# The values of the block-sparse heads: one projection 512 columns wide in the place of two of 256

## The chip, the core and the metric

The kernel runs on one core of a Trainium2 chip. The metric is device time in microseconds (us), the median of several executions. TensorE is the engine that multiplies matrices, VectorE (DVE), ScalarE (ACT) and GpSimd (POOL) do the rest, and each works through its own list of instructions in order.

## The reference

Two transformer blocks run one after the other on 512 tokens of width 1024, in float32. The change is in the first block's projection, of which this is the part that matters:

```python
h = rms_norm(x, norm_mix_pre_g[l])
proj = h @ w_in[l]
mq, mk, mv, dq, dk, dv, ga, gb = jnp.split(proj, split_at, axis=-1)
...
ya = moba_attention(moba_heads(mq), moba_heads(mk), moba_heads(mv), moba_slopes)
...
yb = diff_attention(dq[:, :, 0], dq[:, :, 1], dk[:, :, 0], dk[:, :, 1], dv, lam, diff_slopes)
```

The block-sparse attention (`moba_attention`) has 8 heads of 64 columns, so that `mq`, `mk` and `mv` are 512 columns each. A query attends to its own block of 256 tokens and, where a gate allows, to the block before it. The gate is the sign of the query's product with the mean of the earlier block's keys. The differential attention (`diff_attention`) follows with 4 heads.

## The kernel before

Every product of float32 operands is made of three: each operand is split into a high and a low part (`split`: ScalarE copies the high part, VectorE subtracts it), and `mm3` (lines 371 to 373) adds high·high, high·low and low·high in PSUM. The weights come from memory as slabs. A slab is loaded into a raw tile `wr` (two tiles of 2048 columns) and split in pieces of 1024 columns into tiles `wh` and `wl`, of which there are four pairs (`halves_w`). A slab of 256 columns takes two pieces of four k-blocks each, and a slab of 512 columns takes four pieces of two k-blocks each. The splits of weights are issued at a high priority (`WPRIO`), so that they stand early in the queues of ScalarE and VectorE.

The first block's projections and attention heads share TensorE by a planner, `weave`, that writes TensorE's order down when the kernel is built. It has two lists. *Fills* are projections, taken strictly in the order of their list: `mq`, `mk`, `mv` of half 0 (four heads), the small constants, `mq`, `mk`, `mv` of half 1, then `dq`, `dk`, `dv` of each half, gates, and the branch products. *Chains* are the attention heads: at most three (`WIDTH1`) are active. Each step of a chain states how much it costs and how long the next step has to wait. Whenever a step of an active chain is due, it is taken; otherwise the current fill goes on; and if there is no fill that may start, the planner takes the chain step that comes due first and so TensorE's next instruction is one that waits. A fill may start only when the names that it requires are done: `dq` of half 0 requires `mot` 0 and `mot` 1, the last steps of the first two pairs of heads, because it takes over their tiles.

The heads go in pairs. For a pair p, `moba_open` (`mog`) multiplies the queries by the mean of the keys (line 828, the gate), `moba_head` (`mo`, two for a pair) makes the scores (line 615), the softmax (621 on VectorE, 623 on ScalarE), transposes the probabilities (line 753), splits them, multiplies them by the values (line 883), and folds the result (818, 819). `moba_tail` (`mot`) transposes the sums (line 896) and scales the result (897). `mog` needs `mq` and `mk` of its half, and `mo` needs `mog` and `mv` of its half. The keys' consumer `take_mk` fills the stacked keys on ScalarE and VectorE and then the means (lines 773 and 777), which the gate reads.

The values are projected with the tokens on the partitions: `fill_tok` multiplies each of four groups of 128 tokens by a slab of 256 columns, 24 matmuls a group, with two groups in one PSUM bank; `take_stack_v` then copies and splits the result into stacked tiles (809 and 810).

Of the kernel before, what the change touches and what calls it, by code (L numbers as in the profile page):

```python
# [18 lines left out]
P = 128  # L19
S = 512  # L20
D = 1024
KT = D // P
# [30 lines left out]
CPRIO = 300  # L53
# [24 lines left out]
def STEP(pe=0.0, dve=0.0, act=0.0, ops=(), lat=0.0, free=0, need=0, back=0):  # L78

    return Step(pe, dve, act, ops, lat, free, need, back)
# [11 lines left out]
def transformer_blocks_kernel(  # L94
# [51 lines left out]
    def nm(s):  # L146
        uid[0] += 1
        return f"{s}_{uid[0]}"

    def big(tag, bufs, dt=F32, cols=512):  # L150
        return sp.tile([P, cols], dt, tag=tag, bufs=bufs, name=nm(tag))
# [13 lines left out]
    def acc():  # L165
        return pa.tile([P, 512], F32, tag="a", name=nm("a"))
# [7 lines left out]
    def f32(t):  # L174
        return t.bitcast(F32)
# [90 lines left out]
    def wslab(src, kt, cols, later=None):  # L266
        return list(wpieces(src, kt, cols, later))
# [102 lines left out]
    def mm3(ps, lh, ll, rh, rl, first, last):  # L370
        T.matmul(ps, lh, rh, start=first, stop=False)  # L371
        T.matmul(ps, lh, rl, start=False, stop=False)  # L372
        T.matmul(ps, ll, rh, start=False, stop=last)  # L373
# [12 lines left out]
    def slab_tok(slab, kt, act, ntt, cols):  # L386

        for t in range(ntt):
            if t % 2 == 0:
                bank = acc()  # L390
            ps = bank[:, (t % 2) * 256:(t % 2) * 256 + cols]
            sl = slice(t * P, (t + 1) * P)
            for (k, n, hi, lo) in slab:
                for j in range(n):
                    ah, al = act[k + j]
                    mm3(ps, ah[:, sl], al[:, sl], hi[:, j, :], lo[:, j, :], k + j == 0, k + j == kt - 1)
            yield ps
# [170 lines left out]
    with tc.issue_after(pows[-1].ins):  # L568
        h, ready = pre.operand(w_in[0][:, :256])
# [16 lines left out]
    W1 = w_in[0]  # L586
# [63 lines left out]
    def fill_tok(W, c0, kt, ops, consume, dve, act):  # L650
        held = []
        slab = W if c0 is None else wslab(W[:, c0:c0 + 256], kt, 256)
        for g, ps in enumerate(slab_tok(slab, kt, ops, 4, 256)):
            yield STEP(pe=0.32 * kt, dve=0.28 * kt * (g == 3), act=0.24 * kt * (g == 3))
            held.append((g, ps))
            if g % 2:
                with tc.high_priority(CPRIO):
                    for args in held:
                        consume(*args)
                held = []  # L660
                yield STEP(dve=2 * dve, act=2 * act)

    def weave(chains, fills, width, banks, model):

        hop, bank_lat, fill_lat = model
        now = 0.0
        busy = {"D": [], "A": [], "G": []}  # L670
        done = {}
        banks = [0.0] * banks
        active, todo, queue, cur = [], list(chains), list(fills), None

        def place(engine, t, d):

            spans = busy[engine]
            spans[:] = [sp_ for sp_ in spans if sp_[1] > now]
            k = 0
            while k < len(spans) and spans[k][0] < t + d:  # L680
                t = max(t, spans[k][1])
                k += 1
            spans.insert(k, (t, t + d))
            return t + d

        def take(gen):
            nonlocal now
            st_ = next(gen)
            now += st_.pe
            ready_ = now  # L690
            for e, d in (("D", st_.dve), ("A", st_.act)):
                if d:
                    ready_ = max(ready_, place(e, now + hop, d))
            for ops in st_.ops:
                t = now
                for e, d in ops:
                    t = place(e, t + hop, d)
                ready_ = max(ready_, t)
            banks.extend([ready_ + bank_lat] * st_.free)
            banks.sort()  # L700
            del banks[:max(0, -st_.free)]
            return st_, max(ready_, now + st_.lat)

        def start(c):

            return max(c[2], banks[c[3] - 1] if c[3] else 0.0)

        while active or todo or queue or cur:
            for c in list(todo):
                if len(active) >= width:  # L710
                    break
                name, req, fn = c
                if all(r in done for r in req):
                    todo.remove(c)
                    gen = fn()
                    active.append([name, gen, max([done[r] for r in req] + [0.0]), next(gen).need, []])
            can = [c for c in active if c[3] <= len(banks)]
            due = [c for c in can if start(c) <= now]
            if not due:
                if cur is None and queue and all(r in done for r in queue[0][1]):  # L720
                    name, _, fn = queue.pop(0)
                    cur = [name, fn(), 0.0]
                if cur is not None:
                    try:
                        cur[2] = max(cur[2], take(cur[1])[1])
                    except StopIteration:
                        done[cur[0]] = max(now, cur[2]) + fill_lat
                        cur = None
                    continue
                due = [min(can, key=start)]  # L730
                now = max(now, start(due[0]))
            c = due[0]
            del banks[:c[3]]
            c[3] = 0
            try:
                st_, ready_ = take(c[1])
                c[4].append(ready_)
                c[2] = c[4][-1 - min(st_.back, len(c[4]) - 1)]
                c[3] = st_.need
            except StopIteration:  # L740
                done[c[0]] = c[2]
                active.remove(c)
# [61 lines left out]
    def take_stack_v(key, tag, half):  # L804
        def consume(g, ps):
            v = big(tag, 16, F32R)
            hi, lo = [v.rearrange("p (h u c) -> p h u c", u=2, c=64)[:, :, u] for u in range(2)]
            src = ps.rearrange("p (h c) -> p h c", c=64)
            A.copy(hi, src)
            V.tensor_tensor(lo, src, f32(hi), op=ALU.subtract)  # L810
            for m in range(2):
                store.setdefault((key, half * 2 + m), []).append([v[:, c:c + P] for c in (m * 256, m * 256 + P)])
        return consume
# [216 lines left out]
    fills, chains = [], []  # L1030
    old = []
    for half in range(2):
        tag = "qs"[half]
        c0 = half * 256
        fills.append((("mq", half), old, lambda c0=c0, tag=tag, half=half:
                      fill_feat(W1, c0, take_q("mq", -0.125, tag, half), 1.25, 1.0, DLAT)))
        fills.append((("mk", half), old, lambda c0=c0, tag=tag, half=half:
                      fill_feat(W1, 512 + c0, take_mk(tag, half), 2.4, 2.0, DLAT, half == 0)))
        fills.append((("mv", half), old, lambda c0=c0, tag=tag, half=half:
                      fill_tok(W1, 1024 + c0, KT, h, take_stack_v("mv", tag, half), 0.4, 0.3)))  # L1040
        for p_ in (2 * half, 2 * half + 1):
            chains.append((("mog", p_), [("mq", half), ("mk", half)], lambda p_=p_: moba_open(p_)))
            for hh in range(2):
                chains.append((("mo", p_, hh), [("mog", p_), ("mv", half)],
                               lambda p_=p_, hh=hh: moba_head(p_, hh)))
            chains.append((("mot", p_), [("mo", p_, 0), ("mo", p_, 1)], lambda p_=p_: moba_tail(p_)))
    fills.insert(3, (("gains",), [], fill_constants))
    for half in range(2):
        tag = "qs"[half]
        c0 = half * 256  # L1050
        old = [("mot", 2 * half), ("mot", 2 * half + 1)]
# [8 lines left out]
    for br in range(2):  # L1060
        old = [("di", 0), ("di", 1)] if br == 0 else [("di", hd) for hd in range(4)]
# [109 lines left out]
    h, ready = pre.operand(w_gate[0][:, :256], lambda: mem_slabs(range(0, MEM1)))  # L1171
# [142 lines left out]
    h, ready = pre.operand(ffn1_w_gu_2[0][:, :256], lambda: mem_slabs(range(MEM1, MEM2)))  # L1314
# [20 lines left out]
    h, ready = pre.operand(w_in_2[0][:, 2048:2304], lambda: mem_slabs(range(MEM2, 8)))  # L1335
# [234 lines left out]
    with tc.issue_after(load.ins):  # L1570
# [39 lines left out]
        fills, chains = [], []  # L1610
# [77 lines left out]
    h, ready = pre.operand(mem_w_q_2[0][:, :256])  # L1688


    mo = [None] * KT
# [72 lines left out]
    fills = [(("mq", hd), [], lambda hd=hd: fill_mq(hd)) for hd in range(4)]  # L1764
    fills.append((("mo",), [("ma", hd) for hd in range(3)], fill_mo))
    chains = [(("ma", hd), [("mq", hd)], lambda hd=hd: mem_head(hd)) for hd in range(4)]
# [4 lines left out]
    h, ready = pre.operand(ffn2_w_gu_2[0][:, :256])  # L1771
# [57 lines left out]
```

## Time and profile before

| | us |
|---|---|
| median of 3 runs | 1915.24 |
| lowest and highest | 1912.54, 1916.43 |
| the profiled execution: its time | 1915.45 |
| the profiled execution: its span, first to last instruction | 1913.7 |
| TensorE busy | 1881.5 |
| VectorE busy | 1387.2 |
| ScalarE busy | 929.2 |

The trace is of one execution, whose time of 1915.45 us is 1.75 us more than its span and 0.21 us above the median. Busy time of TensorE is from modelled ends that overlap the next start, so that a stretch without gaps is told better by the starts.

### The profile page before, as it was taken

What the parts mean: (1) busy time and instruction counts of PE and PEld (TensorE: products, weight loads), DVE (VectorE), ACT (ScalarE), POOL (GpSimd) and SP (SyncE); (2) the same over time, 40 slices, a digit from 0 to 9 for tenths busy, and PEclk for the clock granted to TensorE, in tenths of its full rate; (3) what the DMA queues carried; (4) which work ended last, traced back from release to release, by engine and by line L of the source; (5) the groups of instructions that cost most, each with busy time, mean ns of one, the idle gap of its engine ahead of it and who ended that gap; (6) DMA issues with size and microseconds to landing.
All of it is one profiled execution on the core that took longest, in us unless ns stands there. A gap on an engine that the chain in (4) does not pass through costs nothing.

```text
span 1913.7 us, 29312 instructions
## 1 busy us (share of the span) xinstructions
PE 1881.5 (98%) x11566; PEld 1688.7 (88%) x11566; DVE 1387.2 (72%) x2217; ACT 929.2 (49%) x1537; POOL 175.0 (9%) x272
## 2 busy tenths in 40 slices
PE   8999999999999999999999999999999999999998
PEld 7899888888999998889999988888978778999997
DVE  6777635468878786677878757888866448878785
ACT  5666534364544344444344456668555344344443
POOL 2240100050000002000000010330510000000000
PEclk9999999999999999999999999999989999999999
DMA  5221223462232324423232343211223222332322
GB/s 180 67 67 56 78 66 133 143 203 89 89 111 89 114 97 168 151 89 102 97 111 88 111 148 101 67 45 45 89 89 110 77 81 82 102 111 89 111 89 89
DMA packets 161452, 192.40 MB, mean 101 GB/s; under 512 B 7361, under 2 KB 131362, under 8 KB 161314
## 3 DMA queue, kind: packets, MB, share of 16 engines
q1 hardware_dynamic: 159746, 185.80, 29.8%
q0 software_dynamic: 1280, 4.20, 0.6%
q8 instruction: 91, 1.49, 0.3%
q10 hardware_dynamic: 288, 0.52, 0.1%
q14 instruction: 47, 0.39, 0.1%
HBM read 182.11 MB, written 8.39 MB: 100 GB/s over the span
## 4 chain that ended last, share of the span: by engine, by line
PE 88%; issue 5%; DVE 3%; ACT 2%; POOL 2%; POOLq 0%; ACTq 0%; DVEq 0%
PE b L372 16%; PE b L373 16%; PE b L371 16%; PE a L371 11%; PE a L372 11%; PE a L373 11%; PE a L513 4%; PE b L615 1%; PE b L1444 1%; PE b L489 1%; DVE wl L403 1%; PE b L753 1%; DVE w L1540 0%; ACT wh L402 0%; PE b L883 0%
## 5 line engine op out<-in xcount | busy, mean ns | idle before, releaser
L403 DVE TENSOR_TENSOR wl<-wr,wh 128x1024 fp32r<-128x1024 f32 (+1 forms) x381 | 463.5, 1220 | 269.9 <-ACT wh L402 266.1
L402 ACT CAST wh<-wr 128x1024 fp32r<-128x1024 f32 (+1 forms) x381 | 394.0, 1036 | 443.0 <-PE b L372 154.5
L371 PE MATMUL b<-wh,q 128*128 128x512 f32 x672 | 262.4, 390 | 0.0
L372 PE MATMUL b<-wl,q 128*128 128x512 f32 x672 | 262.0, 390 | 0.0
L373 PE MATMUL b<-wh,q 128*128 128x512 f32 x664 | 257.9, 389 | 0.0
L371 PE MATMUL a<-h,wh 128*128 128x512 f32 (+1 forms) x660 | 238.4, 361 | 0.0
L373 PE MATMUL a<-h,wl 128*128 128x512 f32 (+1 forms) x660 | 234.9, 356 | 0.0
L372 PE MATMUL a<-h,wh 128*128 128x512 f32 (+1 forms) x660 | 234.7, 356 | 0.0
L372 PE MATMUL b<-h,wh 128*128 128x256 f32 (+1 forms) x568 | 175.9, 310 | 0.0
L371 PE MATMUL b<-h,wh 128*128 128x256 f32 (+1 forms) x568 | 175.9, 310 | 0.0
L373 PE MATMUL b<-h,wl 128*128 128x256 f32 (+1 forms) x568 | 175.9, 310 | 0.0
L371 PEld LDWEIGHTS b<-wh,q 128*128 128x128 f32 x672 | 126.3, 188 | 24.7
L373 PEld LDWEIGHTS b<-wh,q 128*128 128x128 f32 x664 | 124.6, 188 | 26.5
L372 PEld LDWEIGHTS b<-wl,q 128*128 128x128 f32 x672 | 126.3, 188 | 24.3
L372 PE MATMUL a<-s,wh 128*128 128x256 f32 (+1 forms) x488 | 141.2, 289 | 0.0
L373 PEld LDWEIGHTS a<-h,wl 128*128 128x128 f32 x660 | 124.5, 189 | 18.3
L371 PEld LDWEIGHTS a<-h,wh 128*128 128x128 f32 x660 | 124.7, 189 | 17.9 <-issue 0.5
L372 PEld LDWEIGHTS a<-h,wh 128*128 128x128 f32 x660 | 124.8, 189 | 17.8 <-issue 0.5
L372 PEld LDWEIGHTS b<-h,wh 128*128 128x128 f32 x568 | 108.3, 191 | 5.6
L373 PEld LDWEIGHTS b<-h,wl 128*128 128x128 f32 x568 | 108.2, 191 | 5.6
L371 PEld LDWEIGHTS b<-h,wh 128*128 128x128 f32 x568 | 108.1, 190 | 5.6
L372 PEld LDWEIGHTS a<-s,wh 128*128 128x128 f32 x488 | 93.1, 191 | 1.3
(374 smaller groups left out, 4195.9 us busy)
## 6 DMA issues: line engine op xcount, KB each, us to landing
wr<-in_ffn_w_gu_dram SPq DMA_DIRECT2D x88, 512.0 KB
wr<-in_w_in_dram SPq DMA_DIRECT2D x68, 512.0 KB
wr<-in_ffn_w_down_dram SPq DMA_DIRECT2D x44, 512.0 KB
wr<-in_w_gate_dram SPq DMA_DIRECT2D x22, 512.0 KB
wr<-in_w_up_dram SPq DMA_DIRECT2D x22, 512.0 KB
wr<-in_w_down_dram SPq DMA_DIRECT2D x22, 512.0 KB
wr<-in_mem_w_kv_dram SPq DMA_DIRECT2D x16, 512.0 KB
wr<-in_w_out_dram SPq DMA_DIRECT2D x10, 512.0 KB
```

The lines of the kernel that those rows point to most:

```text
L371: T.matmul(ps, lh, rh, start=first, stop=False)
L372: T.matmul(ps, lh, rl, start=False, stop=False)
L373: T.matmul(ps, ll, rh, start=False, stop=last)
L402: A.copy(hi, src)
L403: V.tensor_tensor(lo, src, f32(hi), op=ALU.subtract)
L489: T.transpose(banks[k][:, t * P:(t + 1) * P], self.s[t, k // 4][:, (k % 4) * P:(k % 4 + 1) * P], ident)
L513: T.matmul(accs[m], lh, rh, start=c == 0 and n in (0, 2), stop=c == KT - 1 and n > 3)
L615: T.matmul(ps, lh[n], rh[n], start=n == 0, stop=n == 1)
L753: T.transpose(ps[:, o * P:(o + 1) * P], blk, ident)
L1444: T.matmul(ps[:, gg * 64:(gg + 1) * 64], e[:, gg * P:(gg + 1) * P], up, start=True, stop=True)
```

## The change

The two fills `mv` of half 0 and half 1 become one fill, in the place of the first. It loads a slab 512 columns wide and multiplies each of the four groups of tokens by it: 24 matmuls of 512 columns a group, each group in a PSUM bank of its own, which the consumers of the two halves read one after the other. All heads now require this one fill. The list of fills has one entry less between `mk` of half 1 and `dq` of half 0.

```diff
+    def fill_both(W, c0, consumes, dve, act):
+
+        slab = wslab(W[:, c0:c0 + 512], KT, 512)
+        for t in range(4):
+            ps = acc()
+            sl = slice(t * P, (t + 1) * P)
+            for (k, n, hi, lo) in slab:
+                for j in range(n):
+                    ah, al = h[k + j]
+                    mm3(ps, ah[:, sl], al[:, sl], hi[:, j, :], lo[:, j, :], k + j == 0, k + j == KT - 1)
+                yield STEP(pe=1.36, dve=1.13 * (t == 3), act=0.95 * (t == 3))
+            with tc.high_priority(CPRIO):
+                for half, consume in enumerate(consumes):
+                    consume(t, ps[:, half * 256:(half + 1) * 256])
+            yield STEP(dve=2 * dve, act=2 * act)
...
-        fills.append((("mv", half), old, lambda c0=c0, tag=tag, half=half:
-                      fill_tok(W1, 1024 + c0, KT, h, take_stack_v("mv", tag, half), 0.4, 0.3)))
+        if half == 0:
+            fills.append((("mv",), old, lambda:
+                          fill_both(W1, 1024, [take_stack_v("mv", "qs"[u], u) for u in range(2)], 0.4, 0.3)))
...
-                chains.append((("mo", p_, hh), [("mog", p_), ("mv", half)],
+                chains.append((("mo", p_, hh), [("mog", p_), ("mv",)],
```

## Rows read from the trace of the kernel before

**Rows 1.** The page's busy times: us (share of the span), instructions.

```profile
PE 1881.5 (98%) x11566; PEld 1688.7 (88%) x11566; DVE 1387.2 (72%) x2217; ACT 929.2 (49%) x1537; POOL 175.0 (9%) x272
```

**Rows 2.** Busy time in stretches of the first block: us busy (instructions), clock, DMA.

```profile
37.22:50.50 13.28, 13.28 (x113) 13.27 (x112) 7.52 (x24) 5.22 (x8) 5.96 (x8) 1.00 0.25 80
50.50:85.16 34.66, 34.66 (x190) 29.99 (x188) 27.51 (x71) 24.53 (x57) 11.36 (x13) 1.00 0.19 61
85.16:101.34 16.18, 15.84 (x131) 15.70 (x130) 11.13 (x32) 8.30 (x15) 4.59 (x6) 1.00 0.21 67
```

**Rows 3.** TensorE's waits in the whole span, this one of 14.

```profile
PE b L828 <- DVE c L777: 0.3, 1, 0.3
```

**Rows 4.** TensorE in order of time, where `mk` of half 0 and `mv` run.

```profile
26.34 0.39 PE L371 MATMUL b<-h,wh 128*128 128x512 f32 x1
...
37.22 0.28 PE L371 MATMUL a<-wh,h 128*128 128x256 f32 x1
...
40.09 0.28 PE L371 MATMUL a<-wh,h 128*128 128x256 f32 x1
```

**Rows 5.** The page's group of weight loads for 512-column products: busy us, mean ns.

```profile
L371 PEld LDWEIGHTS a<-h,wh 128*128 128x128 f32 x660 | 124.7, 189 | 17.9 <-issue 0.5
```

**Rows 6.** VectorE in order of time, a weight piece that `mk` of half 0 frees.

```profile
38.28 1.23 DVE L403 TENSOR_TENSOR wl<-wr,wh 128x1024 fp32r<-128x1024 f32 x1 [0.56 <-ACT wh L402]
```

**Rows 7.** TensorE in order of time from the last `mk` product to `dq`.

```profile
85.16 0.28 PE L371 MATMUL a<-wh,h 128*128 128x256 f32 x1
...
90.91 1.25 PE L753 MATMUL b<-ident,w 128*128 128x128 f32 x10
92.00 0.95 PE L828 MATMUL b<-c,s 128*128 128x1 f32 x8
93.29 1.08 PE L828 MATMUL b<-c,s 128*128 128x1 f32 x8 [0.34 <-DVE c L777]
...
97.18 1.40 PE L883 MATMUL b<-w,q 128*128 128x512 f32 x8
...
101.34 0.60 PE L896 MATMUL b<-ident,w 128*128 128x128 f32 x4
101.70 1.63 PE L615 MATMUL b<-s,s 128*128 128x128 f32 x12
103.16 0.40 PE L371 MATMUL a<-h,wh 128*128 128x512 f32 x1
```

**Rows 8.** VectorE in order of time after the last `mk` product.

```profile
85.18 1.22 DVE L403 TENSOR_TENSOR wl<-wr,wh 128x1024 fp32r<-128x1024 f32 x1
86.31 0.68 DVE L621 CUSTOM_DVE_ANT_0 w<-w,b 128x512 f32<-128x512 f32 x1
...
88.88 1.23 DVE L403 TENSOR_TENSOR wl<-wr,wh 128x1024 fp32r<-128x1024 f32 x1 [0.73 <-ACT wh L402]
...
92.84 0.65 DVE L777 TENSOR_SCALAR c<-c 64x1 f32<-64x1 f32 x4
```

**Rows 9.** ScalarE in order of time, the same stretch.

```profile
87.10 0.72 ACT L623 ACTIVATE w<-w,c 128x512 f32<-128x512 f32 x1 [2.59 <-DVE c L621]
...
87.82 1.03 ACT L402 CAST wh<-wr 128x1024 fp32r<-128x1024 f32 x1
88.75 0.58 ACT L402 CAST s<-a 64x512 fp32r<-64x512 f32 x1
```

**Rows 10.** TensorE in order of time, second block: its longest wait after the start.

```profile
1393.88 1.94 PE L1444 MATMUL b<-w 128*128 128x64 f32 x8 [2.62 <-DVE w L1385]
```

**Rows 11.** Busy time in stretches around that wait; the granted clock stands third from the right.

```profile
1391.00:1392.00 1.00, 0.26 (x2) 0.00 (x0) 0.10 (x1) 0.70 (x4) 1.00 (x4) 1.00 0.45 172
...
1393.00:1394.00 1.00, 0.12 (x1) 0.15 (x1) 1.00 (x5) 1.00 (x3) 0.01 (x1) 0.76 0.03 8
...
1402.00:1403.00 1.00, 1.00 (x4) 0.90 (x4) 0.00 (x0) 0.00 (x0) 0.00 (x0) 0.50 0.00 0
...
1404.00:1405.00 1.00, 1.00 (x10) 1.00 (x10) 0.00 (x0) 0.27 (x2) 0.00 (x0) 1.00 0.00 0
```

## The prediction, made before the run

> **What bounds the kernel now.** I read the busy times first: TensorE is busy for 1881.5 us of a span of 1913.7, VectorE for 1387.2 [rows 1], so TensorE's stream sets the time unless a stage shows otherwise. The stretches of the first block show it stage by stage: while `mv` of half 0 runs, and then `mq` and `mk` of half 1 with the first four heads, TensorE has no gap; in the stretch of `mv` of half 1 it misses 0.34 us of 16.18 [rows 2]. The list of waits names that gap: a gate (line 828) waits for the keys' means from VectorE [rows 3]. That wait is small, and it is the place to look at: it says that VectorE delivers there at the last moment, while TensorE has something else to do. Last I read the three engines in order of time around it.
>
> **The change, part by part.**
>
> *Products.* In a stream of 48 matmuls of 512 columns one starts every (37.22 - 26.34) / 48 = 0.2267 us; in 24 of 256 columns, every (40.09 - 37.22) / 24 = 0.1196 us [rows 4]. Removed are 192 of the narrow ones, 22.96 us; added are 96 of the wide ones, 21.76 us. Gain: 1.2 us. The wide form is another product's, with the operands' roles as in `mk`, but it has the same 128 rows and 512 columns. A gain above this needs a wide pace below 0.2267 us, which is rival 4.
>
> *Weights.* Two slabs of two pieces become one of four, so four loads of 512 KB and four splits stay four. The consumers stay eight copies on ScalarE and eight subtractions on VectorE, 128 by 256 each. This costs nothing as long as the pieces are ready in time. The four pieces take all four pairs of tiles, so the fourth must wait until `mk` of half 0 has ended, at 37.2. Today a piece of the next slab that waits for that same end is subtracted from 38.28 to 39.51 [rows 6]; the fourth piece will be needed after three pieces of six matmuls, at 37.22 + 18 x 0.2267 = 41.3. That leaves 1.8 us. If VectorE is later than that, TensorE waits; a whole split late is 1.2 us (rival 3). The slab after it, `mq` of half 1, takes the first pair when the last group of tokens has used it, 18 x 0.2267 = 4.1 us before the end, and a split is 1.03 us on ScalarE and 1.23 on VectorE [rows 6, 9]: also in time.
>
> *What moves.* `mv` of half 1 leaves the place between `mk` of half 1 and `dq`. Call T the end of `mk`'s last product, 85.16 today, about 10.3 us later afterwards (the earlier fill grows from 11.5 to 21.8 us). From T to the first product of `dq` TensorE now takes 103.16 - 85.16 = 18.0 us [rows 7]: 96 narrow matmuls, 11.48 us; the gate's wait, 0.34; and the rest, 6.18 us, which are ten transposes of the last head of pair 1 (92.00 - 90.91 = 1.09), the gates of pairs 2 and 3, that head's product with the values (1.4 by its row), the tail of pair 1 and the first scores of three heads. The 11.48 us are what covers the waits of these 6.18 us. After the change no fill may go there: `dq` requires `mot` 1, the tail at 101.34, and `mq` and `mk` are done. By the planner's rules TensorE's order will be the chain steps alone, by their due times: transposes of the last head, gate 2, gate 3, that head's product with the values, first scores of heads of pair 2, the tail, a few more scores, and then `dq`.
>
> *When these can run.* The transposes need the last head's exponential, which ScalarE finishes at 87.82 because VectorE starts its part at 86.31, behind a weight piece [rows 8, 9]: T + 2.7. They take 1.09 us and gate 2 takes 0.95. Gate 3 needs the means of pair 3, which VectorE finishes as gate 3 starts, at 93.29, T + 8.1: before them stand two weight pieces, the softmax and the stacked keys [rows 8], and ScalarE reaches the keys only at 88.75, after the exponential and a cast of weights [rows 9]. Nothing in the change shortens this: the weight pieces there are those of `dq`, which take the tiles that `mk` frees, and afterwards those of `dk` will take the tiles that `mk` frees. So TensorE has 1.09 + 0.95 = 2.04 us of work in the first 8.13: a stall of 6.1 us. The lower bound is a VectorE that does the keys ahead of all else: from 88.75 to 93.29 it is 4.54 us, and 4.54 - 2.04 = 2.5 us. The splits of the transposes stand behind the means on VectorE, and while gate 3 runs (1.08 us) only some of them get done; I allow up to 1 us for the product with the values to wait for the rest, and add half of it. I take 5.5 for the gate (near the upper bound, since the queue is today's) and 0.5: 6.0 us, between 2.5 and 7.1. The gate's old wait of 0.34 us is inside it.
>
> *The clock.* TensorE's longest wait after the start is one of 2.62 us in the second block [rows 10]. In the microsecond before its end the granted clock falls to 0.76 and then to 0.50, that is from 2.4 to 1.2 GHz; it is still 0.50 in 1402 to 1403, while TensorE is fully busy, and back at 1.00 in 1404 to 1405 [rows 11]: 10 us at half speed. Ahead of that the engine had been busy and then done nothing. After the change it does nothing for 2.7 us from T, and for 3.4 us between gate 2 and gate 3, so I expect the same. A fall 0.4 us before the end of the second wait, as there, leaves 9.7 us of work at half speed: 4.9 us lost at most, nothing if the clock stays. Part of that stretch lies in waits for the splits anyway, and after a fall in the first wait it ends sooner. I take 3.0.
>
> The Trainium skill ("TensorE: Matmul & The Clock Gate", section "HAM oscillation — how this bites in real kernels") has a rule that speaks against this change: a wait between bursts of matmuls can leave the burst that follows at half the clock. By that rule the sum keeps the 3.0 us, and without it the sum is rival 1; the one fall in this trace [rows 11] agrees with the rule.
>
> *After that.* From `dq` on TensorE has three fills of some 11 us for the four heads of pairs 2 and 3, as today, and those heads have begun a little earlier. I see no new wait there. The first scores that go ahead of `dq` are work moved, at no cost.
>
> *Sum.* 1915.45 (the profiled execution) - 1.2 (products) - 0.3 (the old wait) + 6.0 (stall) + 3.0 (clock) = 1922.9. That execution lies 0.2 us above the median of the runs, so 1922.7; with all bounds taken low, 1915.24 - 1.5 + 2.5 = 1916.2, and with all high, 1915.24 - 1.5 + 7.1 + 4.9 = 1925.7. I forecast 1922.
>
> **The rivals.** About 0.2% of the time, 3.8 us, is what a measurement of this kernel can tell from no change.
>
> 1. *The stall comes, the clock stays.* For it: the two waits are apart, with 2 us of small products between them, and in the second block one row alone shows a fall. Against: that row's wait was no longer. Time: 1915.24 - 1.5 + 2.5 to 7.1, that is 1916.2 to 1920.8, likeliest 1919.7.
>
> 2. *Not slower: the cover is not needed.* The place is the queue of VectorE after T, the price is the stall itself. If the weight pieces and the softmax are set behind the keys, and the last head's exponential is done at T since its biases and scores come earlier, gate 3 waits for no more than the 2 us of work ahead of it. It decides at means that are ready by T + 3.5: then the stall is below 1.5 us and the gain of 1.2 us balances it. VectorE is idle for 0.73 us in this stretch, waiting for a cast [rows 8], so that another order could be quicker; but the keys alone take 4.54 us. Time: 1914 to 1915.5.
>
> 3. *The fourth piece is late.* The stall is hidden as in rival 2, and TensorE waits 1 to 2 us in the first group of `mv`. Against: 1.8 us of margin by today's rows. Time: 1915 to 1917.
>
> 4. *The wide products are faster than the stream before shows,* bounded only by the weight load, 0.189 us [rows 5]: 96 x 0.189 = 18.1 us, a gain of 4.8 us, and 1910.4 with the stall hidden. Against: 48 in a row at 0.2267 us with that same load. The Trainium skill (the same page, section "Back-to-back issue gap") gives 131 ns as the sustained pace of 512-column matmuls in a stream with weight loads; by it the wide products would take 12.6 us (an estimate from that figure) and the gain would be 10.4 us. The trace's 226.7 ns contradicts it.
>
> **How the numbers follow.** The forecast (stall and low clock) has 0.50, with a range of its own from 1918 to 1926; rival 1 has 0.25, rival 2 0.18, rival 3 0.04 and rival 4 0.03. Slower by over 0.2% is above 1919.07: nearly all of the forecast (0.48) and 0.15 of rival 1, together 0.63. Faster by over 0.2% is rival 4, 0.03. The rest, 0.34, is within. The range takes in rivals 1 and 3 and most of 2: 1914.3 to 1925.5.
>
> **What would show it.** In the changed kernel's trace: 96 matmuls of 512 columns at 0.227 us in `mv`, without a gap after the eighteenth; after the last product of `mk` a wait of the transposes for ScalarE and one of the gate for VectorE (line 777), 6 us in all; a granted clock of 0.50 for some 10 us from there; `dq`'s first product 12 us or more after T and not 6. Wrong would be a TensorE without gaps there, a VectorE that finishes line 777 within 4 us of T, a clock that stays at 1.00, or a `dq` that the planner manages to put in between.

## The result, and the profile after

The changed kernel takes 1925.76 us (median of 5 runs, 1923.49 to 1927.47) against 1915.45 us (5 runs, 1912.54 to 1916.43): the ratio is 1.0056 [1.0045, 1.0068]. It is slower, as forecast, but by 10.3 us where the forecast had 7, and it lies 0.3 us above the range. The profiled execution is the one at the median.

The place is the one forecast. The page's busy times of the changed kernel show 96 TensorE instructions fewer, and still 4.9 us more of busy time than [rows 1]:

```profile
PE 1886.4 (98%) x11470; PEld 1687.7 (88%) x11470; DVE 1386.0 (72%) x2217; ACT 929.5 (48%) x1537; POOL 170.9 (9%) x272
```

TensorE of the changed kernel in order of time: start, duration, line, tile, count, and in brackets the idle time before. The new lines stand 16 below the old ones: the gate is 844, the transposes of probabilities 769, the product with the values 899, the tail 912.

```profile
37.47 0.39 PE L371 MATMUL a<-wh,h 128*128 128x512 f32 x1
...
42.91 1.84 PE L844 MATMUL b<-c,q 128*128 128x1 f32 x16
...
95.69 0.49 PE L769 MATMUL b<-ident,w 128*128 128x128 f32 x3
96.67 0.99 PE L769 MATMUL b<-ident,w 128*128 128x128 f32 x7 [0.49 <-ACT w L623]
97.50 0.95 PE L844 MATMUL b<-c,s 128*128 128x1 f32 x8
102.44 1.84 PE L844 MATMUL b<-c,s 128*128 128x1 f32 x8 [3.98 <-DVE c L793]
104.13 2.59 PE L899 MATMUL b<-w,q 128*128 128x512 f32 x8
106.52 3.29 PE L615 MATMUL b<-s,s 128*128 128x128 f32 x12
110.95 1.12 PE L912 MATMUL b<-ident,w 128*128 128x128 f32 x4 [1.14 <-ACT w L908]
111.72 1.20 PE L615 MATMUL b<-s,s 128*128 128x128 f32 x4
112.72 0.63 PE L371 MATMUL a<-h,wh 128*128 128x512 f32 x1
...
139.37 1.02 PE L899 MATMUL b<-w,s 128*128 128x512 f32 x4 [1.11 <-DVE w L403]
141.14 0.91 PE L899 MATMUL b<-w,s 128*128 128x256 f32 x3 [0.75 <-DVE w L403]
...
156.97 0.60 PE L912 MATMUL b<-ident,w 128*128 128x128 f32 x4
157.33 0.36 PE L371 MATMUL a<-wh,h 128*128 128x256 f32 x1
...
420.84 1.36 PE L489 MATMUL b<-ident,y 128*128 128x128 f32 x11
```

The reader is to see five things, each against its row of before.

- `mv`: the 24 wide products of the first group take 42.91 - 37.47 = 5.44 us, 0.2267 us each, as in [rows 4]. All 96 end at 61.08 (with the gates of the first pairs between them).
- T, the end of `mk`'s last product, is 95.69 where it was 85.16. `dq` begins at T + 17.0 where it began at T + 18.0 [rows 7], although 11.48 us of work are gone from between.
- The order in between is the one forecast, and the gate that waited 0.34 us [rows 3] waits 3.98. With the waits of the transposes and of the tail this is 5.6 us.
- At 139 to 142 stand two waits that were not forecast, of the product with the values, for splits on VectorE.
- The last tail of the four heads of half 1 starts at 156.97, and narrow products follow it. These are the rest of `dv` of half 0. In the kernel before, the wide products of the next fill follow it at once, as its TensorE in order of time shows:

```profile
150.18 0.60 PE L896 MATMUL b<-ident,w 128*128 128x128 f32 x4
150.53 0.48 PE L371 MATMUL a<-h,wh 128*128 128x512 f32 x1
...
405.43 1.25 PE L489 MATMUL b<-ident,y 128*128 128x128 f32 x10
```

The transposes of line 489 stand ahead of the first feed-forward part. I take the start of the first of them as the end of the stretch that the change can touch: 405.43 before, 420.84 after, 15.4 us later.

The busy times of the changed kernel in stretches (PE, PEld, DVE, ACT, POOL, then the granted clock) show the clock that goes with it:

```profile
37.47:61.08 23.61, 23.61 (x113) 19.76 (x112) 11.56 (x30) 8.83 (x14) 9.15 (x12) 1.00 0.14 45
...
95.69:112.72 17.03, 11.41 (x55) 10.41 (x54) 10.91 (x40) 8.63 (x21) 7.91 (x11) 0.63 0.19 64
...
99.00:100.00 1.00, 0.00 (x0) 0.00 (x0) 1.00 (x2) 0.95 (x3) 0.00 (x0) 1.00 0.07 14
100.00:101.00 1.00, 0.00 (x0) 0.00 (x0) 0.94 (x3) 0.94 (x3) 0.00 (x0) 0.60 0.88 251
...
116.00:117.00 1.00, 1.00 (x4) 0.71 (x4) 0.62 (x2) 0.03 (x1) 0.00 (x0) 0.50 0.00 0
117.00:118.00 1.00, 1.00 (x6) 0.91 (x5) 0.84 (x5) 0.82 (x2) 0.00 (x0) 0.86 0.00 0
...
143.00:144.00 1.00, 1.00 (x4) 0.80 (x3) 0.59 (x2) 0.38 (x2) 0.00 (x0) 0.50 0.00 0
```

It falls from 1.00 to 0.50 (2.4 to 1.2 GHz) at 100.2, in the gate's wait (0.60 as the mean of that microsecond), and is back at 117.3. At 141.2 it falls once more, for 3.4 us.

**Why 15.4 us there are 10.3 at the end.** From 405.43 to the second block TensorE's starts are moved by the same amount in both traces, within 0.3 us. The whole difference after that arises in one place. One stretch of the second block, between its first and second group of line 489, takes 298.87 us before (1132.54 to 1431.41) and 294.08 after (1147.68 to 1441.76), which gives 4.8 us back. The work in it is the same. What differs is where the clock falls: in the kernel before from 1393 to 1404 [rows 11], in the changed one at 1370, for 3.4 us. Over the runs below this stretch takes from 294.07 to 298.87 us, with no relation to the edit that I could find, and executions of one kernel differ too: narrow_half_products, below, ran from 1910.12 to 1916.10 us, with the short stretch in the profiled execution, the quickest. So a median carries up to 5 us that the edit did not cause, and I compare the experiments by the end of the first stretch as well, which does not contain it. That end has a spread of its own: the first product of `mv`, ahead of which no edit changes the work, starts between 37.00 and 38.42 in the profiled executions, so that differences of about 1 us between two ends say little.

### The profile page after: what moved, and what is told of

The parts are those of the page before. It is cut to its first block, busy times and chain, and to the rows that moved or that the text cites. A ratio compares the mean times of both kernels' runs of the same rounds, so it can differ in the third digit from the quotient of the medians.

```text
span 1924.1 us, 29119 instructions
## 1 busy us (share of the span) xinstructions
PE 1886.4 (98%) x11470; PEld 1687.7 (88%) x11470; DVE 1386.0 (72%) x2217; ACT 929.5 (48%) x1537; POOL 170.9 (9%) x272
## 4 chain that ended last, share of the span: by engine, by line
PE 87%; issue 5%; DVE 4%; ACT 2%; POOL 1%; POOLq 0%; ACTq 0%; DVEq 0%
PE b L372 16%; PE b L373 15%; PE b L371 15%; PE a L371 11%; PE a L372 11%; PE a L373 11%; PE a L513 4%; PE b L1461 1%; PE b L615 1%; PE b L489 1%; DVE wl L403 1%; PE b L769 1%; DVE w L1557 1%; ACT wh L402 0%; PE b L899 0%
## 5 line engine op out<-in xcount | busy, mean ns | idle before, releaser
L372 PE MATMUL a<-s,wh 128*128 128x256 f32 (+1 forms) x488 | 141.2, 289 | 0.0
```

## The experiments

My theory at first was the prediction's: TensorE stands still behind T, and the clock falls. The rivals were that the width costs something, that the heads of half 0 start too late, and, when these had fallen, that the heads' time and the work that TensorE may do beside them were in balance and the change upsets the sum. That last reading is only partly shown, as the experiments below say. The table has the markers of every profiled execution, and the ratio of each kernel to runs of the kernel before on the same chip. *T*: end of `mk` of half 1. *Heads*: from T to the last tail of half 1, as TensorE's list has it. *Rest*: from that tail to the first line 489, which is 255.3 us where the tail is followed by the fill that followed it before, 8.6 us more where 72 narrow products of `dv` are left over (72 x 0.1196 = 8.6), and less where products of `dq` of half 1 have run ahead of the tail. *End*: that first line 489 against 405.43.

| kernel | T | heads | rest | end | median | ratio |
|---|---|---|---|---|---|---|
| before | 85.16 | 65.0 | 255.3 | | 1915.45 | |
| after | 95.69 | 61.3 | 263.9 | +15.4 | 1925.76 | 1.0056 [1.0045, 1.0068] |
| narrow_both_first | 96.70 | 60.2 | 263.9 | +15.3 | 1928.85 | 1.0069 [1.0057, 1.0081] |
| narrow_first_heads_early | 101.77 | 62.9 | 255.3 | +14.5 | 1928.90 | 1.0074 [1.0062, 1.0086] |
| wide_warm_gate | 95.76 | 61.2 | 263.9 | +15.4 | 1925.87 | 1.0055 [1.0043, 1.0067] |
| wide_idle_fill | 96.49 | 58.8 | 263.9 | +13.7 | 1927.07 | 1.0064 [1.0052, 1.0076] |
| wide_early_dq | 95.42 | 63.8 | 256.1 | +9.9 | 1924.89 | 1.0045 [1.0033, 1.0057] |
| wide_both_dq_early | 95.28 | 65.7 | 247.6 | +3.1 | 1917.92 | 1.0013 [1.0005, 1.0022] |
| wide_gate_fill | 95.50 | 59.9 | 263.7 | +13.7 | 1925.75 | 1.0060 [1.0048, 1.0073] |
| narrow_few_products | 84.97 | 63.3 | 255.3 | -1.9 | 1911.42 | 0.9978 [0.9969, 0.9987] |
| narrow_half_products | 85.09 | 64.6 | 255.3 | -0.5 | 1915.05 | 0.9994 [0.9986, 1.0003] |
| narrow_more_products | 84.95 | 70.3 | 255.3 | +5.1 | 1917.38 | 1.0015 [1.0006, 1.0024] |
| wide_means_first | 95.51 | 57.9 | 263.9 | +11.8 | 1923.55 | 1.0053 [1.0041, 1.0065] |
| wide_bias_no_gate | 96.08 | 58.0 | 263.9 | +12.6 | 1922.97 | 1.0040 [1.0028, 1.0053] |
| wide_both_dq_paced | 95.47 | 76.7 | 245.9 | +12.7 | 1927.07 | 1.0069 [1.0056, 1.0082] |
| wide_paced_means_first | 96.66 | 77.3 | 245.9 | +14.5 | 1927.70 | 1.0066 [1.0053, 1.0079] |

### Is it the width, or when the first heads begin?

**narrow_both_first**: the kernel before with its two narrow fills, both in the place of the first, and all heads behind both.

```diff
+        for u in range(2 * (half == 0)):
+            fills.append((("mv", u), old, lambda c0=u * 256, tag="qs"[u], half=u:
+                          fill_tok(W1, 1024 + c0, KT, h, take_stack_v("mv", tag, half), 0.4, 0.3)))
...
-                chains.append((("mo", p_, hh), [("mog", p_), ("mv", half)],
+                chains.append((("mo", p_, hh), [("mog", p_), ("mv", 1)],
```

> Both fills of values stay 256 columns wide, as in the kernel before, but both stand ahead of mq of half 1, and all heads wait for both, as in the changed kernel; only the width of the products is undone. If the loss is the missing cover between mk of half 1 and dq (waits and half clock there), the time is that of the changed kernel plus the 1.2 us of the products, 1925 to 1929, and the gate of pair 3 waits some 4 us for VectorE. If the wide products or the slab that takes all four pairs of weight tiles cost the time, it comes back to 1914 to 1917.

It ends at +15.3, and the median is 1928.85 us, within the range: the whole loss, without one wide product. From the first product of `mv` to the transpose of line 233 behind the last, its two fills take 24.81 us (37.25 to 62.06) and the wide one 23.61 (37.47 to 61.08). These 1.20 us are the gain that *Products* had worked out. **narrow_first_heads_early** is the same, but heads require `("mv", half)` as before and so start after the first fill.

> As the run before it, but the heads of half 0 wait for the first of the two narrow fills alone, so that they begin one fill earlier, while the second is still being multiplied. If the loss is that the last head of pair 1 is not finished when the fills run out, the heads now have a fill more of time and the wait after mk is gone: 1914 to 1917, clock 1.00 there. If a fill of values ahead of mq costs the time wherever the heads begin (the rival), it is 1924 to 1928.

It ends at +14.5, and its median of 1928.90 us lies 0.9 above the rival's range. The heads of half 0 come earlier, and the gate of half 1 still waits for line 777 (3.4 us). So neither the width nor the start of the first heads costs the time; moving the fill does.

### Is it the standstill behind T, and the clock?

**wide_warm_gate**: 16 matmuls with no consumer ahead of the last gate.

```diff
             gp = aux()
+            if p_ == 3:
+                for n in range(16):
+                    T.matmul(gp, h[0][0][:, :P], h[0][0], start=True, stop=True)
```

> The changed kernel with 16 extra products of 512 columns, read by nothing, between the two gates of pairs 2 and 3, 3.6 us of TensorE work inside its wait of 4.0 us for VectorE. The wait for VectorE is left as it is. If the half clock after that wait is a part of the loss, as 13 us of work between 102.4 and 117.2 at 0.50 say, the clock stays at 1.00 there and the time falls by 4 to 7 us, to 1919 to 1922. If the waits alone make the loss (the rival), the time stays at 1925 to 1927.

TensorE in order of time, and its busy times:

```profile
98.38 3.94 PE L844 MATMUL b<-h 128*128 128x512 f32 x16
102.41 1.17 PE L847 MATMUL b<-c,s 128*128 128x1 f32 x8
...
111.05 1.12 PE L915 MATMUL b<-ident,w 128*128 128x128 f32 x4 [4.45 <-ACT w L911]
```

```profile
105.00:110.00 5.00, 1.61 (x12) 1.28 (x11) 2.45 (x10) 1.42 (x5) 4.49 (x6) 1.00 0.01 2
110.00:115.00 5.00, 3.95 (x14) 3.47 (x15) 3.12 (x11) 2.84 (x11) 4.37 (x5) 0.54 0.00 0
```

The gate no longer waits and the clock stays at 1.00 until 110. Then the tail waits 4.45 us for ScalarE, at 111.05 where it started at 110.95, and the clock falls there. The end is the same to 0.02 us, and the median is in the rival's range; the wait had only stood in another place.

One thing more stands in the rows of the changed kernel: what holds the tail of pair 1. It waits for a copy on ScalarE (line 908). The sums which that copy reads are ready at 96.85, but in ScalarE's list it stands behind three exponentials of pair 2. These wait for VectorE, and VectorE for the biases of GpSimd, which begin at 104.12, after the gate. VectorE, GpSimd, VectorE and ScalarE in order of time:

```profile
96.65 0.20 DVE L906 RECIPROCAL c<-c 128x8 f32<-128x8 f32 x1 [0.94 <-ACT w L623]
104.12 0.48 POOL L870 TENSOR_SCALAR w<-dist,c 128x256 f32<-128x256 f32 x1 [11.99 <-issue]
107.52 0.43 DVE L874 SCALAR_TENSOR_TENSOR w<-dist,w 128x256 f32<-128x256 f32 x1 [1.69 <-POOL w L872]
109.03 0.40 ACT L623 ACTIVATE w<-w,c 128x128 f32<-128x128 f32 x1 [1.69 <-DVE c L621]
...
110.30 0.60 ACT L908 COPY w<-c 128x512 f32<-128x512 f32 x1
```

In the kernel before, the same copy runs ahead of those exponentials, and is done 5.6 us before the tail at 101.34 [rows 7]:

```profile
95.14 0.62 ACT L892 COPY w<-c 128x512 f32<-128x512 f32 x1
```

So the tail, and `dq` which requires it, come behind work of pair 2 through the order of ScalarE's list. Without the wait for the gate (wide_bias_no_gate, below) the copy still runs at 110.25, behind the same exponentials, which then wait for the fold of the product with the values. No run moves this copy, so what its place costs is open.

**wide_idle_fill**: a fill ahead of `dq`, of 96 narrow products that nobody uses, 11.5 us, as long as the one that was moved away.

```diff
+    def fill_pad():
...
+            for k in range(KT):
+                mm3(ps, h[k][0][:, t * P:(t + 1) * P], h[k][1][:, t * P:(t + 1) * P],
+                    h[k][0][:, :256], h[k][1][:, :256], k == 0, k == KT - 1)
+            yield STEP(pe=2.56)
...
+    fills.append((("pad",), [], fill_pad))
```

> The changed kernel with a fill of 96 products of 256 columns, read by nothing, between mk of half 1 and dq, 11.5 us of TensorE work in the place that mv of half 1 had. If the second half's heads need their time whatever TensorE does, the extra work is free: 1924 to 1928, no waits there and a clock of 1.00. If the waits after mk are a matter of TensorE's order alone and can be had back, extra work must cost a good part of its 11.5 us: 1930 to 1937.

Its busy times:

```profile
95.00:115.00 20.00, 20.00 (x160) 19.57 (x159) 12.11 (x39) 8.47 (x20) 8.76 (x12) 1.00 0.17 54
115.00:160.00 45.00, 43.12 (x252) 37.19 (x251) 31.43 (x69) 28.00 (x60) 7.93 (x11) 1.00 0.15 48
```

There is no gap behind T until 139, where the two waits for splits remain (1.9 us), the clock is at 1.00 throughout, and the end is +13.7; the median is in the range set for heads that need their time. The other waits and all of the low clock behind T are worth 1.7 us more than 11.5 us of useless work, or 2.5 us counted from the first product of `mv`, which starts 0.8 us later here. Taking the standstill away thus gains little: TensorE's time is lost there whether it waits or works for nothing, and what is missing is useful work that may run there.

### Is it the work that may run beside the heads?

**wide_early_dq** lets `dq` and `dk` of half 0 start before the tail of pair 1.

```diff
+        soon = [("mot", 0), ("mk", 1)] if half == 0 else old
-        fills.append((("dq", half), old, lambda c0=c0, tag=tag, half=half:
+        fills.append((("dq", half), soon, lambda c0=c0, tag=tag, half=half:
```

> The changed kernel with one requirement less: dq and dk of half 0 wait for the tail of pair 0 and for mk, no longer for the tail of pair 1, so that a fill stands again after mk of half 1. If the missing cover is the cause, TensorE waits less than 1 us there, the clock stays at 1.00, and the gain of 1.2 us of the wide products is left: 1913 to 1916. If the wide form is the cause: 1924 to 1927.

Its busy times:

```profile
95.00:115.00 20.00, 19.51 (x108) 16.72 (x107) 12.79 (x42) 10.40 (x23) 9.69 (x12) 1.00 0.17 54
...
155.00:160.00 5.00, 3.60 (x20) 3.01 (x18) 2.63 (x11) 2.45 (x9) 0.00 (x0) 0.64 0.59 200
```

The hole behind T is full, with waits of 0.5 us there and a clock of 1.00, and no `dv` is left over: 5.5 us better. The forecast of the time missed all the same. The median, 1924.89 us, even lies in the range set for the wide form as the cause, which narrow_both_first excludes. For now the three fills run out before the heads do: at 152 to 160 TensorE waits, the clock falls, and the end is +9.9. **wide_both_dq_early** goes a fill further: the values of half 1 go into a ring of tiles that is free there (`"qy"[u]` for `"qs"[u]`), so that `dq` of half 1 needs only `("mk", 1)`.

> wide_early_dq with one thing more: the values of half 1 lie in four tiles of their own (of the ring y), so that dq of half 1 need not wait for the tails of pairs 2 and 3 and TensorE has a fill while the last heads finish. If TensorE lacked fills while the second half's heads took their time, the loss is now gone: 1913 to 1917. If the loss is in the time of VectorE and the others, which no order of fills shortens: 1921 to 1926.

It ends at +3.1, and is 0.13% slower than the kernel before, 0.9 us above the range of the theory. TensorE's waits between 50 and 405 are now these, 3.7 us in all (waits, times, longest):

```profile
PE b L769 <- ACT w L623: 1.9, 2, 1.6
PE b L769 <- DVE w L403: 1.3, 1, 1.3
PE b L912 <- ACT w L908: 0.3, 1, 0.3
PE b L844 <- DVE c L793: 0.2, 1, 0.2
```

**wide_gate_fill** fills the hole from elsewhere: one projection of the gates, 10.9 us of products that ran beside the differential heads, is taken at T (`EGAT = (6, 20)` for `(14, 20)`, results in that free ring).

> The changed kernel with the first projection of the gates (256 columns, 10.9 us of TensorE work, which requires nothing) taken from behind dv of half 1 to the place between mk of half 1 and dq; its two results lie in tiles of the ring y. The cover is real work again. If the missing cover there is the cause, the waits after mk go, the clock stays at 1.00, and the first block ends 0 to 4 us after 405.4, some of the cover being missed at the differential heads now: 1914 to 1919. If the loss is elsewhere, as wide_early_dq could also be read: 1923 to 1927.

Behind T TensorE is full at clock 1.00, as its busy times show first. But the end is +13.7, and the median is in the range set for a loss elsewhere. The lack comes back where the work was taken from: a wait of 4.2 us that ends at 207.68 (TensorE in order of time), and a low clock.

```profile
95.00:115.00 20.00, 19.81 (x112) 17.24 (x112) 11.57 (x40) 10.00 (x22) 9.69 (x12) 1.00 0.17 54
...
220.00:225.00 5.00, 4.10 (x15) 3.74 (x16) 3.83 (x17) 1.86 (x7) 1.27 (x1) 0.50 0.00 0
```

```profile
207.68 3.42 PE L769 MATMUL b<-ident,w 128*128 128x128 f32 x17 [4.22 <-DVE w L947]
```

### How near was the balance before?

Three kernels change the length of `mv` of half 1 in its old place, in the kernel before, and move nothing. **narrow_few_products** leaves out 84 of its 96 products (only `k == 0` and `h[0]` are done), **narrow_half_products** 48 of them (`for j in range(0, n, 2)`), so that the values of half 1 are incomplete in both; **narrow_more_products** adds 48 that nobody uses:

```diff
+            for k in range(4):
+                mm3(ps, h[k][0][:, sl], h[k][1][:, sl], h[k][0][:, :256], h[k][1][:, :256], k == 0, k == 3)
```

> The kernel before, with 84 of the 96 products of mv of half 1 left out (so that these values are not the reference's); order, splits and consumers stay. 10.0 us of TensorE work go from the stretch between mk of half 1 and dq, and nothing is put anywhere else: what the change takes away there, alone. If the second half's heads need their own time, the first block ends where it does before (405.4) or less than 3 us earlier, and the time is 1912 to 1916. If the work's place mattered only through some waits, the first block ends 5 to 10 us earlier: 1905 to 1910.

> The kernel before, with every second k-block left out of the products of mv of half 1 (48 of 96 matmuls, so that these values are not the reference's); order, splits and consumers stay. It takes 5.7 us of TensorE work out of the stretch between mk of half 1 and dq. Theory: once the keys of half 1 are there, the second half's heads need a time of their own, some 62 to 66 us to their last tail as in the runs so far, which TensorE only fills; then the time stays at 1913 to 1916 and waits appear. Rival: TensorE sets the end of this stage before the change, and only special waits lengthen it afterwards; then it is 1908.5 to 1910.5.

> The kernel before, with 48 extra products of 256 columns, read by nothing, ahead of those of mv of half 1: 5.7 us more of TensorE work at the place where narrow_half_products has 5.7 us and narrow_few_products 10.0 us less. If TensorE and the heads are in balance before the change, each us added costs a us while each us taken away gives almost nothing: the first block ends 5 to 6 us later (411; 405.4 before), 1920 to 1922. If there is still room, so that the heads set the end of the stage, under 2 us: 1914 to 1917.

Against 10.0 us of work taken away stand 1.9 us at the end, against 5.7 us 0.5 us; but 5.7 us added cost 5.1. The first two ends are as the theory had them, and so is the third; the medians lie 0.6 us below its range, within it, and 2.6 us below it, the last with a short stretch in the second block (295.74 us). TensorE's waits, first with few products and then with half of them, show where the saving went:

```profile
PE b L849 <- DVE c L798: 3.7, 1, 3.7
PE b L774 <- ACT w L623: 1.6, 1, 1.6
```

```profile
PE b L849 <- DVE c L798: 3.2, 1, 3.2
```

The gate's wait takes it, and the clock that falls in it. With half of the products the gate starts at 93.22, where it started at 93.29 before; it waits 2.9 us more, and then 5.0 us of work run at half speed, 2.5 lost:

```profile
93.22:98.22 5.00, 5.00 (x22) 4.90 (x23) 3.72 (x16) 1.37 (x3) 1.84 (x3) 0.50 0.28 93
```

Together that is 5.4 of the 5.7 us. With few products the waits give 4.9 us more and the half clock 3.3, together 8.2 of 10.0. With more products TensorE has no wait at all between 50 and 400. So the kernel before stood at a corner: TensorE reached the gate when the means did. Work taken from this place is worth almost nothing, work added to it costs nearly its full length.

That the heads' whole length is what holds the end is not shown by this. ScalarE is done with its part of the last tail long before that tail starts, 7.6 us in the kernel before and 5.4 in the changed one:

```profile
141.96 0.62 ACT L892 COPY w<-c 128x512 f32<-128x512 f32 x1
```

```profile
150.94 0.61 ACT L908 COPY w<-c 128x512 f32<-128x512 f32 x1
```

So the last tails at 150.18 and 156.97 stand where TensorE's list has them, and the column *heads* is a length of that list.

### What sets the time from T to the last tail?

**wide_means_first** puts the means ahead of the stacked keys in `take_mk`:

```diff
-            store["mk", p_] = stack_k(ps, tag)
             ksum = col(1)
...
             store["kmean", p_] = kmean
+            store["mk", p_] = stack_k(ps, tag)
```

> The changed kernel with the keys' means computed ahead of the stacked keys in take_mk, the same instructions in another order. The gate of pair 3 should wait 2 to 3 us less. If that gate's wait and the clock after it are the loss, the time falls to 1917 to 1921. If the heads' time as a whole counts, it falls by no more than the 2 to 3 us by which the gates come earlier: 1922 to 1925.

The gate's wait is gone, the tail waits 3.25 us instead, and the heads take 57.9 us, 3.4 less; the median is in the second range. **wide_bias_no_gate** gives the biases of half 1, which GpSimd makes from the gate's result, a constant in place of that result:

```diff
+            e0c, s1c, s2c = [t[:, c:c + 1] if p_ < 2 else mhalf[:, c:c + 1] for t in (e0, s1, s2)]
```

> The changed kernel in which GpSimd's biases for the heads of pairs 2 and 3 read constants in the place of the gate's result, so that the output is not the reference's; the instructions and their sizes stay. GpSimd can then make the first biases while it waits for the gate today (89 to 104 us). If the chain from the keys' means over the gate and GpSimd's biases to the softmax sets the second half's time, VectorE no longer waits 3.9 us for GpSimd, and the first block ends 3 to 6 us earlier than in the changed kernel (its operand transposes before the first feed-forward start at 420.8 there): 1919 to 1923 in all. If VectorE's own list of work sets it, under 1 us: 1924.5 to 1926.5.

The heads take 58.0 us, the end is 2.8 us earlier, and the median is in the first range. In the changed kernel's waits behind T (95 to 120), VectorE's softmax waits for those biases:

```profile
DVE w L874 <- POOL w L872: 4.5, 4, 1.7
```

Each of the two edits thus gains some 3 us, and neither alone brings the loss back. That the chains themselves became shorter by as much is not shown: TensorE's waits from T to the last tail add up to 7.3 and 7.1 us, against 7.5 in the changed kernel. What shrank is the low clock, from 20.5 us to 10.2 and 13.7, without a fall near 141.

Last, I tried to close the 3.1 us that wide_both_dq_early leaves. **wide_both_dq_paced** tells the planner that a step of the heads of half 1 takes 3 us longer (`lat=MOLAT + 3.0 * (p_ > 1)`), to spread them over the fills; **wide_paced_means_first** adds the means first.

> wide_both_dq_early, with 3 us more given to the planner as the wait after the later scores of pairs 2 and 3, so that the transposes come later than the exponentials they read. Its two waits of 3 us in all should go, and with the 1.2 us of the wide products the first block should end 0 to 2 us before the kernel before does (405.4; 408.5 in wide_both_dq_early): 1913 to 1916. If the heads' time is still the bound, new waits take their place: 1917 to 1919.

> wide_both_dq_paced with the keys' means ahead of the stacked keys. With TensorE covered there is little left to gain from earlier gates: within 1 us of wide_both_dq_paced, 1912 to 1916.

Both missed their ranges by over 8 us; only the second's nearness to the first, 0.6 us, is as expected. The heads became 11 us longer (76.7 and 77.3), and the last tail waits 4.3 us for ScalarE in both. No wide version beats the kernel before.

## Why the prediction failed in its size

The mechanism was right, and two terms of the sum failed: *The clock*, and *After that*, which was put at nothing.

- *Products* was right: 0.2267 us each, and 1.2 us measured between narrow_both_first and the changed kernel for 1.2. Rival 4 falls.
- *Weights* was right: no product of `mv` waits, and VectorE's row of the fourth piece has it done at 39.76, where it was needed at 37.47 + 18 x 0.2267 = 41.6. Rival 3 falls.

```profile
38.53 1.23 DVE L403 TENSOR_TENSOR wl<-wr,wh 128x1024 fp32r<-128x1024 f32 x1 [0.59 <-ACT wh L402]
```

- *What moves* and *When these can run* were right in the order, and nearly in the size: 5.6 us of waits for 6.0. The part after the gate fell on the tail (1.14 us, ScalarE), not on the product with the values. That the size came so near is partly luck. The tail's place behind pair 2's exponentials was not seen, and the half clock filled most of that wait: at a clock of 1.00 the tail waits 4.45 us (wide_warm_gate). Rival 2 falls.
- *The clock* was right in its mechanism and mis-sized: 3.0 us, at most 4.9, and 6.8 measured. I let the clock come back after 10 us, as in [rows 11]; it stayed at 0.50 from 100.2 to 117.3, with the rest of the gate's wait and the tail's inside. Of these 17.1 us the waits are 3.4, so 13.7 us of work ran at half speed, and 6.8 were lost. Rival 1 falls.
- *After that* is the other step that failed: "three fills of some 11 us for the four heads of pairs 2 and 3, as today ... I see no new wait there". It stood in the sum at nothing. Measured are 3.6 us: two waits of 1.9 us for splits at 139 and 141, and 1.7 us for a second fall of the clock. I treated TensorE as if from `dq` on it would run without a gap and at full clock, as before.

With these two terms the sum closes. Before, 64.7 us of TensorE's work stood in the 65.0 us from T to the last tail ([rows 7] has T). In the changed kernel TensorE does 11.5 us (`mv`) and 8.6 us (`dv` left over) less between T and the last tail, so 64.7 - 20.1 = 44.6 us of work stand in 61.3 us: 16.7 us are lost. By the terms they are 5.6 (waits behind T), 6.8 (clock), 1.9 (the second waits) and 1.7 (the second fall of the clock), together 16.0; 0.7 us has no name. The prediction had 9.0. Its 7.5 us for the first block and the 15.4 measured differ by 7.9, of which 7.7 are this loss. In the whole time the miss is smaller, 10.3 us for 7, only because the second block gave 4.8 us back, which the prediction had not foreseen; that is luck.

But wide_idle_fill and wide_warm_gate show that these terms are not separate prices: where one is cured, another takes its time. What these kernels share is that `dq` has to wait for the tail of pair 1: it starts 16 to 19 us after T in every kernel with the heads behind all of `mv` and the requirement kept, with the hole or without, and from T to the last tail pass 58 to 61 us, while T is some 10.5 us later. Of the 15.4 us, 5.5 lie in the order of the work (`dq` may not start, wide_early_dq), and another 6.8 in too little work that may run before the heads end (wide_both_dq_early against wide_early_dq); 3.1 are left, with waits of 3.7 us.

Three things stay open. Why 58 to 61 us pass from T to the last tail is only half told: the two edits tried gain 3 us each, and both at once were not run. What the copy's place in ScalarE's list costs was not tried. And neither was why the stretch of the second block has more than one length.

## What to carry to other kernels

Where projections fill the gaps of attention chains, ask of each fill what would wait if it were not there, and which work may run in its place by its requirements. If none may, moving the fill to a place without gaps costs its length there and gives little back where it was: here 11.5 us moved cost 15.4, though no work was added. The hole that opens is not a price by itself: filled with work of no use, or with work borrowed from the next such stretch, it left the end within 2 us of where it was; useful work that was allowed to start earlier brought 12.3 us back. To see this before a change, shorten the fill in place; if its saving does not appear at the end, its cover is worth more than its speed. And follow a wait on another engine to its place in that engine's list: the input of the tail's copy was ready 13 us before the copy's turn came.

## What the runs showed of the hardware

After the gate's wait of 3.98 us the clock stayed low for 17.1 us, with a second wait of 1.14 us inside; after the wait of 2.62 us in the kernel before, for 10 us [rows 10, 11]; in narrow_half_products, with a wait of 3.2 us, for 6.8. The length of a fall could thus not be taken over from one row. The Trainium skill ("TensorE: Matmul & The Clock Gate", section "HAM oscillation — how this bites in real kernels") says that a wait can return a burst to the low clock each time anew. The fall at 100.2, in the gate's wait, agrees with it. The fall at 141.2 followed waits of only 1.11 and 0.75 us, and after the same two waits in wide_idle_fill the clock stayed at 1.00. Products that nobody uses held it there (95 to 160), and this bought little time.
